# Other slot counts for the experts of a mixture-of-experts layer: 28 units of 128 slots in place of 32, in another order

## The chip, the cores and the metric

The program runs on one core of a Trainium2 chip. The metric is device time in microseconds (us) of one execution; smaller is better. Three runs of the kernel before took 2062.28, 2062.32 and 2063.19 us, so the median is 2062.32 us.

## The reference

Two transformer blocks on 256 tokens of 1024 features, in float32. The change concerns only the last part, the mixture of experts: each token goes to 8 of 64 experts, and each expert is a small gated network.

```python
def _moe(h, w_router_l, bias_l, w_gate_l, w_up_l, w_down_l, w_sh_gate_l, w_sh_up_l, w_sh_down_l):
    xt = h.reshape(t, d)                                     # 256 tokens x 1024
    scores = jax.nn.sigmoid(xt @ w_router_l)                 # 64 experts, in 8 groups
    biased = scores + bias_l
    # the best 4 groups, in them the best TOP_K = 8 experts: sel; weights from scores, summing to 2.5
    ...
    def expert_block(args):
        xe, e = args
        return (jax.nn.silu(xe @ w_gate_l[e]) * (xe @ w_up_l[e])) @ w_down_l[e]   # 1024 -> 256 -> 1024
    yb = lax.map(expert_block, (xb, block_e))
    routed = jax.ops.segment_sum(yb * slot_w, slot_tok)      # weighted sum per token
    shared = (jax.nn.silu(xt @ w_sh_gate_l) * (xt @ w_sh_up_l)) @ w_sh_down_l
    return routed + shared
```

An expert has 3 MB of weights (1024x256 gate, 1024x256 up, 256x1024 down), so the 64 experts bring 201 MB from HBM, whatever the routing.

## The kernel before

`route` scores the experts and sorts them by their load, which is the number of tokens that chose them. "Place" j is the j-th in that order; the first PRE = 2 places are always the experts 0 and 1, so that their weights can be loaded before the router is done. The later places' expert numbers are read into registers of the SyncE queue (L1772) and used as addresses of the loads.

The number of slots (tokens that an expert can take) is fixed when the program is built, by the place. TIERS says from which place on how many: 128 slots from place 0, 64 from place 12, 32 from place 40. If an expert had more tokens than its slots, `overflow` would send every token through every expert in a loop; a count on the chip decides that.

Slots are handled in **groups** of 256 and **units** of 128. A group is 2 experts of 128 slots, 4 of 64 or 8 of 32; each group is two units. For a group, `gather` copies the tokens of the 256 slots into columns with one-hot products on TensorE (tiles `oh`, `tok` to `xg`: 32 products of 128x256). For a unit, `experts` multiplies the gathered columns with the gate and up weights, 8 k-tiles for each expert, 512 columns each, into one PSUM tile (`pd<-ring,xg`). An expert of 64 or 32 slots uses 64 or 32 columns of TensorE's array and its own part of the output's partitions. `tail` makes the unit's scatter matrix and slot weights (`slT`, `w`), the activation (`tg`, then `h`), two transposes (`cst,h`, L1858), and the down products with 4 times 512 columns for each expert (`pm<-ring,hT`). `scatter` adds a group's two units to the output with 16 products (`pm<-y,PT`).

So a unit costs 12 float32 products of 512 columns for each of its 1, 2 or 4 experts. In the profile a float32 product of these shapes is two instructions (two passes), and is counted twice; gather and scatter products are one.

All expert weights come through one ring of NRING = 25 tiles of 128x1024 (512 KB), loaded by SyncE in the order of use (`ring`, L1576). An expert is 6 tiles: 4 of gate and up (`in_w_gu`), 2 of down (`in_w_ed`). Load k waits until the tile of load k - 25 has been used.

ORDER lists the tiers of the groups in the order in which they are taken. While a group's gate and up products run, `pump` puts in steps of the tail and scatter of the unit before and of the gather of the next group. A scheduler then fixes the order of instructions on each engine when the program is built, by its own estimate of when data arrive; the engine runs them in that order.

```python
TIERS = ((0, 128), (12, 64), (40, 32))
ORDER = (0, 2, 0, 0, 1, 1, 0, 1, 1, 0, 1, 2, 0, 1, 1, 2)
```

```python
m = P // nu                                   # columns of one expert in a unit of nu experts
for kk in range(2):
    k = 2 * c + kk
    for i, w in enumerate(ws):
        s0 = U["s0"] + i * m
        self.mm(U["ps"][i * m:(i + 1) * m], st["x"][:, k, s0:s0 + m], w[:, kk * 512:(kk + 1) * 512], k == 0, k == KD - 1)
```

Of the kernel before, what the change touches and what calls it, by code (L numbers as in the profile page):

```python
# [28 lines left out]
# ----------------------------------------------------------------- constants (of the shapes alone)  # L29
# [13 lines left out]
# places in the order by load: the first PRE are the experts 0.., then from each place on so many slots for each expert  # L43
PRE = 2
# lengths of streams, for the proportion in which they are merged
NCTX, PAD = 64, 4
NLAT, NWIN, NCONV = 70, 45, 120
# tiles of gates, of weights ahead; k-tiles that the vector engine takes; the group beside the shared expert's last product
# [4 lines left out]
TIERS = ((0, 128), (12, 64), (40, 32))  # L53
# the tiers of the groups of 256 slots, in the order in which they are taken
ORDER = (0, 2, 0, 0, 1, 1, 0, 1, 1, 0, 1, 2, 0, 1, 1, 2)
# [5 lines left out]
def _consts():  # L61
# [3 lines left out]
    # additive masks, queries on partitions  # L65
# [4 lines left out]
    # [partition t, free i]  # L70
# [4 lines left out]
    # within 32 rows and columns, lower and upper: the second block of a pair of s rows, the first of s columns  # L75
# [30 lines left out]
    # rope rows: 0..31 cos, 32..63 sin (with the sign), twice  # L106
# [23 lines left out]
# ----------------------------------------------------------------- layout of the inputs  # L130


def _pack(w, ncol):
    """(K, C) -> (C/ncol, 128, K/128 * ncol)"""
    k, c = w.shape
    return np.ascontiguousarray(w.reshape(k // P, P, c // ncol, ncol).transpose(2, 1, 0, 3)).reshape(c // ncol, P, -1)


def _cols(v):
    """(n*128,) -> (128, n)"""  # L140
    return v.reshape(-1, P).T
# [5 lines left out]
def _layout(inp):  # L147
# [50 lines left out]
    # second block  # L198
# [34 lines left out]
# ----------------------------------------------------------------- kernel  # L233


class Kern:
# [12 lines left out]
    # -------- streams of instructions: generators that yield where another stream may come in  # L249
# [20 lines left out]
    @staticmethod  # L270
    def merge(*streams):
        """streams: (generator, its number of steps); all advance in proportion"""
        live = [[g, 0, n] for g, n in streams]
        while live:
            e = min(live, key=lambda e: e[1] / e[2])
            e[1] += 1
            if next(e[0], StopIteration) is StopIteration:
                live.remove(e)
            yield

    # -------- small helpers
# [3 lines left out]
    def mm3(self, out, L, R, n, start=True, stop=True):  # L285
        """out = sum over n k-tiles of L[k]^T R[k]; L, R: (hi, lo) callables of k"""
# [19 lines left out]
    def split(self, hi, lo, src, lo_eng=None):  # L306
        """hi + lo = src exactly, each with at most 12 significant bits"""
        self.act(hi, src, AF.Copy)
        self.tt(lo, src, hi.bitcast(F32), ALU.subtract, lo_eng)

    def wraw(self, src, n):
        """src [128, n] in DRAM, loaded"""
# [6 lines left out]
    def wload(self, src, n, pre=True):  # L319
        """src [128, n] in DRAM -> hi, lo [128, n]"""  # L320
# [25 lines left out]
    # -------- setup  # L346
# [67 lines left out]
    def t5_bias(self, tp):  # L414
        """bias tiles [128 q, 8 heads, keys] with the masks added"""
# [5 lines left out]
        # differences of neighbouring buckets; bucket 0 keeps its value  # L421
# [4 lines left out]
        # three exact bf16 parts, block-diagonal over the key groups  # L426
# [12 lines left out]
        for b in range(2):  # L439
            nk = 32 if b == 0 else 64  # L440
            ng = 4 * nk
            for h0 in range(0, nk, 16):
# [10 lines left out]
                # ps columns (k, g, h) -> bias[q, h, g * nk + h0 + k]  # L453
# [6 lines left out]
    # -------- 1/sqrt(src * scale + eps), [128, n] for small n  # L460
# [13 lines left out]
    def rows(self, cols, dst):  # L474
        """dst [128, 256] = cols [128, 2] (tokens on partitions) as a row on every partition"""
# [6 lines left out]
    def rstd(self, sqs, n, name, dst=None):  # L482
        """1/sqrt(mean + eps) over the partitions of the [128, 256] tiles sqs: (columns [128, 2], rows [128, 256])"""
# [7 lines left out]
    def rstd_rows(self, sqs, n, tmp):  # L491
        """rows of 1/sqrt(mean + eps) over the partitions, worked out on every partition; tmp [128, 4, 256]"""
# [5 lines left out]
    def add_sq(self, acc, k, x, eng=None, **kw):  # L498
        """acc (+)= x^2, the first k writing it"""
# [10 lines left out]
    # -------- dense products; activations (hi, lo) [128, KT, 256]; calls cb(f, psum [128, n * 256], n)  # L510
# [3 lines left out]
    def dense_g(self, src, kt, nt, X, cb, m=P, kparts=1, per=1, pair=2):  # L514
        """out^T, features on partitions: nt tiles of m features. src(i): chunk i in DRAM [128, kt * per * m];
        kparts chunks of kt k-tiles each add up to one output, or one chunk holds per outputs.
        X: hi, lo, or one tile in float32"""
# [28 lines left out]
    # -------- softmax attention over up to 256 keys; score(b, h, ps) emits the products  # L546
    def attention(self, mp, *a):
        """stream: vtok [128, 2, w] tokens on partitions; head h's values at columns vcol(h); Y hi, lo [128, 4, 256]"""
# [47 lines left out]
    # -------- one layer of the first block  # L596
    def mix(self, l, XG, r):
        """x += mixer(x); hi, lo of x^T * g_mlp and the row of r^2 of its norm"""
        tp = lambda n: self.tc.tile_pool(name=f"{n}{l}", bufs=1, reuse_waits="tile")
        with tp("q") as qp:  # L600
# [7 lines left out]
            # output projection (the gates' halves come in here), residual  # L608
# [13 lines left out]
    def ff(self, l, XM, r, fp, res):  # L622
        """x += mlp(x), in two halves of the hidden features; res: the next XG and sums of squares"""
# [31 lines left out]
    def queries(self, l, XG, r, qp):  # L655
        """projections of the sliding-window attention"""
# [22 lines left out]
    def mixer(self, l, XG, Q, mp):  # L679
# [4 lines left out]
        # convolution branch: GLU, then the taps  # L684
# [20 lines left out]
        # sliding-window attention  # L705
# [9 lines left out]
        # latent attention: projections and norms of the latents  # L715
# [25 lines left out]
        # gates (tanh: 2 * sigmoid - 1) and the gated sum of the branches, which takes the first gate's place  # L741
# [15 lines left out]
        def branch(n, Y, f, gate):  # L757
            """outputs f, f + 1 of branch n"""
# [11 lines left out]
        # latent attention  # L770
# [50 lines left out]
        # layer norm over channels, swish  # L821
# [32 lines left out]
    def residual(self, k, X, g, acc, eng=None):  # L854
        """after x^T tile k is final: hi, lo of x*g and its part of the sum of squares"""
# [6 lines left out]
    # ---------------------------------------------------------------- second block  # L862
# [11 lines left out]
    def modulation(self, js, mp):  # L874
        """stream: parts js of the modulation, as columns [128, 8] each; 0, 1 for the context too (columns 48..63)"""
# [39 lines left out]
    def modulated(self, x, r, a, b, X, pool):  # L915
        """hi, lo of x * r * a + b; r rows, a and b columns per k-tile"""
# [6 lines left out]
    def decays(self, pool):  # L923
        """powers of the retention's decays: columns"""
# [8 lines left out]
    def decay_tables(self, pool):  # L933
        """DT [128 j, 4, 128 i], both directions; rows of powers"""
# [14 lines left out]
    def tr4(self, dst, srcs, scale=None):  # L949
        """dst [128, 4, 128] = transposes of four [128, 128] tiles, times scale(i) [128, 1]"""  # L950
# [11 lines left out]
    def rope2(self, dst, ps, f, scale, pool):  # L962
        """dst [128, 2, 256] = rotated ps (two heads), times scale"""
# [8 lines left out]
    def short_conv(self, z, ps, tile0, pool):  # L972
        """z [128, 2, 256] = 2 * silu(conv(ps)) of two channel tiles"""
# [12 lines left out]
    def l2(self, zs, pool, kt, ktok, mul):  # L986
        """z = 2 * silu; kt [128, 4, 256] (channels on partitions) and ktok [128, 2, 4, 128] of the normalised heads, times mul"""
# [12 lines left out]
    def state_features(self, X, base, pool, rope, F):  # L1000
        """stream: the features that feed the states, into the dict F"""
# [27 lines left out]
        # the decay gates first  # L1029
# [14 lines left out]
    def gdn_gates(self, p3, la, be, pool):  # L1044
        """la = -exp(a_log) * softplus(p + dt_bias), be = sigmoid(p)"""
# [6 lines left out]
        # softplus(x) = max(x, 0) + log1p(exp(-|x|)); log1p(e) = 2 atanh(e / (2 + e))  # L1052
# [16 lines left out]
    def b4(self, x):  # L1069
        """[128, 4] -> [128, 4, 128]"""  # L1070
        return x[:, :, None].to_broadcast([P, 4, P])
# [4 lines left out]
    def retention_kv(self, F, d, n, pool, kv):  # L1076
        """kv [PSUM 128 d, (4, 128 e)] of chunk n, direction d"""
# [12 lines left out]
    def gdn_prep(self, F, d, n, pool, kk, qk, G):  # L1090
        """stream: for chunk n in direction d the decays and the inverse of I + A, transposed, into the dict G;
        kk (and qk): the keys' products where A (the output's weights) may differ from 0"""
# [20 lines left out]
        # A, queries on partitions  # L1113
# [12 lines left out]
        # X, the inverse of I + A^T, and Y = X^T: blocks of 2 up to 32 in 32 columns, by X <- X - X B X  # L1126
# [28 lines left out]
        # the larger blocks: a, b the first and the second of a pair  # L1155
# [36 lines left out]
    def gdn_step(self, F, G, n, s_old, s_new, pool, o):  # L1192
        """stream: one chunk: s_new (None: not wanted) from s_old (None: zero); o: (output tile, whether to write or add)"""
# [42 lines left out]
    def context(self, c2):  # L1236
        """stream: states after the context: retention and delta rule, both directions"""
# [37 lines left out]
    def gdn_preps(self, F, pool, out, G):  # L1275
        """stream: gdn_prep for both directions of both chunks"""
# [24 lines left out]
    def head_norm(self, o, mean, pool):  # L1301
        """in place over the last axis of o [128, 2, 4, 128]: (o - mean) / sqrt(var + eps) or o / rms"""
# [14 lines left out]
    def final_norm(self, accs):  # L1317
        """rows of 1/rms of the first block's end, and of it times the next norm's, from sum((x g_final)^2)"""
# [24 lines left out]
    def mixer2(self, r1, r12, rffn):  # L1343
        nc, A, two, x = self.nc, self.A, self.two, self.xT
        tp = lambda n: self.tc.tile_pool(name=n, bufs=1, reuse_waits="tile")
        with tp("mb") as base:
# [7 lines left out]
            with tp("m1") as pool:  # L1354
# [19 lines left out]
                # retention: states, then the chunks  # L1374
# [29 lines left out]
            # delta rule  # L1404
            with tp("m2") as pool:
# [9 lines left out]
                # gates of the heads and of the merge beside it  # L1415
# [17 lines left out]
    def logits_x(self):  # L1433
        """the router's logits are r2 (x + r1 og) f_a W + f_b W: the parts of x and of f_b, and f_a W"""
# [16 lines left out]
    def mix_out(self, X, ro, go, rg, gz, gates, pool, rffn, wr, lx):  # L1451
        nc, A, two, x = self.nc, self.A, self.two, self.xT
        gates.append(pool.tile([P, 8, S], F32, name="gates1"))
        # norms over the heads, gates, transposed
# [14 lines left out]
        # merge; the factors 1/2 of silu and of the gates make 1/4  # L1469
# [13 lines left out]
        # og: the output o times its norm's gain; sums over the features of o^2, og^2 and og x  # L1483
# [41 lines left out]
        with self.tc.high_priority():  # L1525
            # sum((x + r1 og)^2) = sum(x^2) + r1 (2 sum(og x) + r1 sum(og^2))
# [540 lines left out]
```

## Time and profile before

| | us |
|---|---|
| median of three runs | 2062.32 |
| span of the profiled execution | 2062.9 |
| experts' stage, from the first product on an expert's weights to the last scatter | 1458.2 to 2050.3 |
| after it, last norm and store | 2050.3 to 2062.9 |

The profile gives no other time of the profiled execution than its span, which is 0.6 us above the median. Times in the rows are counted from the span's start. A TensorE instruction's end is modelled and overlaps the next, so what an instruction costs is read from the start of one row to the start of the next.

### The profile page before, as it was taken

The page shows a single profiled execution, that of the slowest core. Times are in us where ns is not written, and L with a number is a line of the kernel's source. Part 1 is how long each engine was busy: PE and PEld are TensorE (multiplying, and loading weights), DVE is VectorE, ACT ScalarE, POOL GpSimd, SP SyncE. Part 2 cuts the span into 40 slices and gives each one's busy share as a digit, 9 for nine tenths or more (in the row PEclk, how much of TensorE's full clock was granted, in tenths as well). Part 3 has the DMA queues.
Part 4 walks back from the last instruction along what each step waited for, and adds up shares of the span by engine and source line. Part 5 has one row for each costly group of instructions (what it writes and reads, how often), then busy time and mean ns, then how long its engine had stood idle before and what let it go on. Part 6 is the DMA issues. An engine that isn't in the chain of part 4 may idle for free. (4 is left out here: it accounts for less than half of the span.)

```text
span 2062.9 us, 38136 instructions
## 1 busy us (share of the span) xinstructions
PE 1900.5 (92%) x15189; PEld 1512.5 (73%) x15189; DVE 1272.2 (62%) x2464; ACT 786.7 (38%) x1397; POOL 292.4 (14%) x216
## 2 busy tenths in 40 slices
PE   5888999999888999998988998996999999999996
PEld 5787999999787999998987988895645443433432
DVE  7999787887986688578657864487222222222223
ACT  3246555344257555444444433352212121121111
POOL 3433210001334220011131121103000000000000
PEclk9989999999989999999989997896999999999998
DMA  4423556776423567655523522154798988889994
GB/s 160 124 82 113 171 177 201 244 245 200 134 76 106 176 202 228 210 172 172 156 91 96 161 91 65 33 180 186 264 409 305 353 276 304 283 287 409 348 349 197
DMA packets 122149, 414.49 MB, mean 201 GB/s; under 512 B 13936, under 2 KB 14832, under 8 KB 121968
## 3 DMA queue, kind: packets, MB, share of 16 engines
q1 hardware_dynamic: 120528, 409.92, 58.7%
q8 instruction: 120, 1.97, 0.4%
q10 hardware_dynamic: 1440, 2.11, 0.3%
q14 instruction: 61, 0.50, 0.1%
HBM read 410.92 MB, written 1.05 MB: 200 GB/s over the span
## 5 line engine op out<-in xcount | busy, mean ns | idle before, releaser
L283 PE MATMUL pd<-X,whi 128*128 128x256 f32 (+2 forms) x3280 | 639.3, 294 | 19.6 <-DVE X L304 9.8
L283 PEld LDWEIGHTS pd<-X,whi 128*128 128x128 f32 (+2 forms) x3280 | 534.0, 198 | 25.9 <-DVE X L304 11.7
L292 ACT ACTIVATE whi<-raw 128x1024 fp32r<-128x1024 f32 x340 | 356.4, 1051 | 458.7 <-PE pd L283 341.2
L283 PE MATMUL pd<-X,wlo 128*128 128x256 f32 (+2 forms) x1640 | 480.0, 293 | 8.2 <-POOL wlo L295 4.6
L295 DVE TENSOR_TENSOR wlo<-raw,whi 128x1024 fp32r<-128x1024 f32 x286 | 357.5, 1253 | 130.7 <-ACT whi L292 125.7
L283 PEld LDWEIGHTS pd<-X,wlo 128*128 128x128 f32 (+2 forms) x1640 | 324.7, 198 | 12.2 <-POOL wlo L295 6.1
L283 PE MATMUL pd<-ring,xg 128*64 128x512 f32 (+2 forms) x1024 | 284.3, 602 | 0.0
L283 PE MATMUL pd<-H,whi 128*128 128x256 f32 x1024 | 188.4, 286 | 0.3 <-ACT H L292 0.3
L295 DVE TENSOR_TENSOR y<-pm,y 128x512 fp32r<-128x512 f32 x64 | 44.2, 691 | 209.6 <-ACT y L292 209.5
L283 PEld LDWEIGHTS pd<-ring,xg 128*64 128x64 f32 (+2 forms) x1024 | 78.3, 136 | 113.4 <-issue 105.3
L295 POOL TENSOR_TENSOR wlo<-raw,whi 128x1024 fp32r<-128x1024 f32 (+1 forms) x54 | 132.6, 2470 | 197.6 <-ACT whi L292 197.2
L283 PEld LDWEIGHTS pd<-H,whi 128*128 128x128 f32 x1024 | 159.4, 192 | 1.1 <-ACT H L292 0.5
L283 PE MATMUL pm<-ring,hT 128*64 128x512 f32 (+2 forms) x512 | 153.7, 601 | 1.6 <-ACT hT L292 1.6
L304 DVE SCALAR_TENSOR_TENSOR cv<-up,vec,cv 128x256 f32<-128x256 f32 x240 | 148.1, 656 | 0.2
L283 PE MATMUL pd<-H,wlo 128*128 128x256 f32 x512 | 145.2, 284 | 0.4 <-DVE wlo L295 0.4
L304 DVE SCALAR_TENSOR_TENSOR acc<-rawm,sl,acc 128x512 f32<-128x512 f32 x112 | 94.1, 855 | 22.6 <-DMA rawm<-in_w_mod 22.2
L292 ACT ACTIVATE y<-pm 128x512 fp32r<-128x512 f32 (+1 forms) x66 | 39.4, 597 | 171.4 <-PE pm L283 171.4
L283 PEld LDWEIGHTS pd<-H,wlo 128*128 128x128 f32 x512 | 98.1, 192 | 0.8 <-DVE wlo L295 0.8
L283 PEld LDWEIGHTS pm<-ring,hT 128*64 128x64 f32 (+2 forms) x512 | 42.1, 136 | 75.1 <-issue 66.8
L283 PEld LDWEIGHTS pm<-oh,tok 128*128 128x128 f32 x512 | 67.2, 189 | 35.0 <-issue 29.3
L295 POOL TENSOR_TENSOR sqacc<-sqacc,sq 128x256 f32<-128x256 f32 x42 | 37.7, 905 | 366.0 <-ACT sq L292 364.9
L283 PE MATMUL pm<-oh,tok 128*128 128x256 f32 x512 | 87.3, 306 | 1.8 <-DVE oh L295 1.8
(515 smaller groups left out, 2721.6 us busy)
## 6 DMA issues: line engine op xcount, KB each, us to landing
ring<-in_w_gu SPq DMA_DIRECT2D x256, 512.0 KB, 6.8
ring<-in_w_ed SPq DMA_DIRECT2D x128, 512.0 KB, 8.5
raw<-in_w_up SPq DMA_DIRECT2D x64, 512.0 KB, 4.3
raw<-in_w_dn SPq DMA_DIRECT2D x64, 512.0 KB, 4.3
raw<-in_w_g SPq DMA_DIRECT2D x48, 512.0 KB, 3.6
rawm<-in_w_mod SPq DMA_DIRECT2D x96, 256.0 KB, 3.5
raw<-in_w_s SPq DMA_DIRECT2D x32, 512.0 KB, 3.7
raw<-in_w_x SPq DMA_DIRECT2D x32, 512.0 KB, 3.5
```

Source lines behind the costliest of these rows:

```text
L283: return self.nc.tensor.matmul(out, l, r, start=start, stop=stop)
L292: self.nc.scalar.activation(out, in_, f, **kw)
L295: (eng or self.nc.vector).tensor_tensor(out, a, b, op)
L304: self.nc.vector.scalar_tensor_tensor(out, a, s, b, op0, op1)
```

## The change

Two tables of constants. (The change also removes comments and docstrings, which leave blank lines behind, so that all line numbers stay.)

```diff
-TIERS = ((0, 128), (12, 64), (40, 32))
-# the tiers of the groups of 256 slots, in the order in which they are taken
-ORDER = (0, 2, 0, 0, 1, 1, 0, 1, 1, 0, 1, 2, 0, 1, 1, 2)
+TIERS = ((0, 128), (8, 64), (32, 32))
+
+ORDER = (0, 2, 0, 1, 1, 2, 0, 1, 1, 2, 0, 1, 1, 2)
```

| | experts before | units before | experts after | units after |
|---|---|---|---|---|
| 128 slots | 12 | 12 | 8 | 8 |
| 64 slots | 28 | 14 | 24 | 12 |
| 32 slots | 24 | 6 | 32 | 8 |
| all | 64 | 32 (16 groups) | 64 | 28 (14 groups) |

TensorE's order is the same up to the start of the fourth group, which is now one of 64 slots; the rows below are the first that differ (names: `pd` sums of gate and up, `ring` weights, `xg` gathered tokens, `hT` transposed activation, `oh`,`tok` gather).

```order
 L283 MATMUL pd<-ring,xg 128x512 x2
 L1858 MATMUL pm<-cst,h 128x128 x2
-L283 MATMUL pd<-ring,xg 128x512
+L283 MATMUL pd<-ring,xg 64x512
 L283 MATMUL pm<-ring,hT 128x512 x4
-L283 MATMUL pd<-ring,xg 128x512
-L283 LDWEIGHTS idb
-L283 MATMUL pm<-slT,idb 128x256
-L283 MATMUL pm<-oh,tok 128x256 x8
```

What moved: where a product of the next 128-slot expert stood, one of a 64-slot expert stands.

TensorE before, in the first unit of the second 32-slot group (the 12th group): a part of its gate and up products.

```order
L283 MATMUL pd<-ring,xg 32x512
L1858 MATMUL pm<-cst,h 128x128 x2
L283 MATMUL pm<-oh,tok 128x256 x8
L283 MATMUL pd<-ring,xg 32x512 x13
L283 MATMUL pm<-ring,hT 64x512
L283 MATMUL pm<-oh,tok 128x256 x7
L283 MATMUL pm<-ring,hT 64x512 x3
L283 MATMUL pm<-oh,tok 128x256
L283 MATMUL pd<-ring,xg 32x512 x8
L283 MATMUL pm<-ring,hT 64x512
```

TensorE now, in the second 32-slot group (now the 6th group): the second half of the first unit's gate and up products, and the first two of the second unit.

```order
L283 MATMUL pd<-ring,xg 32x512 x2
L1858 MATMUL pm<-cst,h 128x128 x2
L283 MATMUL pd<-ring,xg 32x512 x14
L283 MATMUL pm<-ring,hT 64x512 x5
L283 MATMUL pm<-y,PT 128x512 x4
L283 MATMUL pm<-ring,hT 64x512 x3
L283 MATMUL pm<-y,PT 128x512 x5
L283 MATMUL pd<-ring,xg 32x512
L283 MATMUL pm<-y,PT 128x512 x5
L283 MATMUL pd<-ring,xg 32x512
```

What moved: the 32-wide products still stand in stretches of several, broken by gather, scatter and down products, and some stand alone, but the stretches are cut in other places.

## Rows read from the trace of the kernel before

**Rows 1.** The page's first line.

```profile
span 2062.9 us, 38136 instructions
```

**Rows 2.** Stretches: us, then busy us (x instructions) per engine, granted clock, DMA share, GB/s.

```profile
1458.20:1516.80 58.60, 58.07 (x339) 27.03 (x337) 13.32 (x35) 14.80 (x27) 0.00 (x0) 1.00 0.85 307
1516.80:1555.10 38.30, 38.30 (x132) 17.03 (x132) 10.50 (x20) 4.65 (x10) 0.00 (x0) 1.00 1.03 409
...
1618.00:1652.50 34.50, 34.50 (x160) 14.30 (x156) 8.33 (x17) 7.22 (x14) 0.00 (x0) 1.00 1.01 378
...
1827.50:1884.60 57.10, 54.20 (x304) 19.80 (x303) 15.55 (x39) 9.80 (x19) 0.00 (x0) 1.00 0.88 337
1884.60:1918.20 33.60, 33.60 (x114) 14.00 (x113) 8.56 (x16) 4.95 (x9) 0.00 (x0) 1.00 1.03 409
1918.20:1950.10 31.90, 31.90 (x142) 13.72 (x141) 7.96 (x17) 5.67 (x11) 0.00 (x0) 1.00 0.91 338
1950.10:1988.80 38.70, 38.70 (x165) 15.07 (x164) 9.37 (x20) 6.64 (x14) 0.00 (x0) 1.00 0.91 326
1988.80:2050.30 61.50, 56.52 (x322) 20.20 (x322) 17.25 (x38) 11.22 (x23) 0.00 (x0) 1.00 0.74 286
2050.30:2062.90 12.60, 0.43 (x2) 0.00 (x0) 7.71 (x34) 1.95 (x6) 0.00 (x0) 0.55 0.23 86
```

**Rows 3.** Who TensorE, its weight loads and SyncE's queue waited for, 1458 to 2050.

```profile
PE pm L1858 <- DVE h L295: 6.1, 6, 1.7
...
PEld pd L283 <- DMA ring<-in_w_gu: 1.1, 2, 0.8
...
SPq L1576 <- PE pd L283: 173.9, 102, 9.2
SPq L1576 <- PE pm L283: 95.9, 90, 3.4
SPq L1576 <- DMA ring<-in_w_gu: 53.4, 75, 2.0
```

**Rows 4.** DMA in the same stretch.

```profile
DMA packets 52022, 189.77 MB, mean 321 GB/s; under 512 B 5776, under 2 KB 5776, under 8 KB 51984
```

**Rows 5.** TensorE in order of time, 128 slots: start, us, operation, passes.

```profile
1560.56 1.20 PE L283 MATMUL pm<-oh,tok 128*128 128x256 f32 x8
1561.61 0.30 PE L283 MATMUL pm<-w,ohb 128*128 128x1 bf16 x6
...
1571.79 1.10 PE L283 MATMUL pm<-y,PT 128*128 128x512 f32 x4
1572.73 1.88 PE L283 MATMUL pd<-ring,xg 128*128 128x512 f32 x4
...
1584.13 3.60 PE L283 MATMUL pm<-ring,hT 128*128 128x512 f32 x8
1587.56 2.89 PE L283 MATMUL pd<-ring,xg 128*128 128x512 f32 x10
```

**Rows 6.** The same, 64 slots.

```profile
1615.43 1.07 PE L283 MATMUL pd<-ring,xg 128*64 128x512 f32 x2
1616.43 0.30 PE L283 MATMUL pm<-w,ohb 128*128 128x2 bf16 x6
1616.66 1.94 PE L283 MATMUL pd<-ring,xg 128*64 128x512 f32 x8
1618.53 0.44 PE L1858 MATMUL pm<-cst,h 128*128 128x128 f32 x2
```

**Rows 7.** The same, 32 slots.

```profile
1870.05 3.64 PE L283 MATMUL pd<-ring,xg 128*32 128x512 f32 x32
1873.50 2.74 PE L283 MATMUL pm<-ring,hT 128*32 128x512 f32 x18
...
1877.17 1.04 PE L283 MATMUL pm<-ring,hT 128*32 128x512 f32 x2
1878.15 0.39 PE L283 MATMUL pm<-oh,tok 128*128 128x256 f32 x1
```

## The prediction

> **What bounds the kernel now.** The page's span is 2062.9 us [rows 1]; the change touches the experts' stage alone, so the next view is the sum by stretches, cut at the starts of groups [rows 2]. It shows TensorE busy in practically all of each stretch, at a granted clock of 1.00 (the upper of its two levels, 2.4 GHz), VectorE and ScalarE below half. DMA is busy too, 0.74 to 1.03. Which of the two sets the time is told by the waits [rows 3]: TensorE's weight loads waited 1.1 us for gate and up tiles; SyncE's queue waited 270 us for TensorE to free ring tiles (two rows), and in 75 places, 53 us, for an earlier load. So the loads wait for TensorE, hardly ever the reverse. TensorE works in a fixed order, so the stage, 2050.3 - 1458.2 = 592.1 us, is what that order costs.
>
> **What an instruction costs**, from one row's start to the next. A float32 product of 512 columns on the whole array: (1587.56 - 1584.13) / 4 = 0.86 us (8 passes are 4 products) [rows 5]. Experts of 64 slots: 8 passes, 4 products, take 1.87 us, so two run beside each other [rows 6]. Experts of 32 slots: 32 passes, 16 products, take 3.45 us, so four run beside each other [rows 7]. I call 0.86 us a *turn*: one product of 128 slots, up to two of 64, up to four of 32. A product that stands alone takes a whole turn: 1.00 us for 64 [rows 6], 0.98 for 32 [rows 7], 0.12 of it for the change of column width, or 0.11 a change with what the next instruction loses. A gather product takes 1.05 / 8 = 0.13, a scatter product 0.94 / 4 = 0.235 [rows 5].
>
> **The change, part by part.** Products by kind: 12 a unit and expert gave 144, 336 and 288 (128, 64, 32 slots), now 96, 288 and 384; the shared expert's 8 stay. If all ran in full turns, that would be 152 + 168 + 72 = 392 turns before and 104 + 144 + 96 = 344 after. But the order breaks the stretches. Counting in the order of both built programs (neighbours that write different partitions share a turn) gives 152 + 199 + 105 = 456 before and 104 + 178 + 136 = 418 now.
>
> - Turns: 38 fewer by 0.86 = -32.7 us.
> - Gather, two groups of 32 products: 64 by 0.13 = -8.3.
> - Scatter, two groups of 16: 32 by 0.235 = -7.5.
> - One-hot rows, slot weights and transposes of four units, at some 0.6 a unit by the short rows [rows 5, 6]: -2.5.
> - Changes of column width: 337 to 331, by 0.11: -0.7.
> - Waits for the activation `h` before the transposes, 6.1 us in 6 places now [rows 3]. They come where little stands between the slot weights (`w`) and the transposes, as in 32-slot units. Such places number five before and nine after in the order; two of the new ones have more cover than the old. At some 0.7 each: +2.8.
>
> Sum: -48.9 us. As a test, the same list prices the whole old order: 456 turns 392, gather 480 by 0.13 = 62, scatter 256 by 0.235 = 60, small ones 22, changes 37, together 574 of the 592.1 traced. The 18 left are waits, mostly in the last group, which is alike in both.
>
> ScalarE and VectorE lose two groups' evacuations; they are off the path, so that is worth nothing. The number of bytes is the same, and so are SyncE's loads of registers, one for each expert past the second. The last norm, 12.6 us, and all before the stage keep their order.
>
> Bounds. From above: piece the new sequence together from old stretches with the same neighbours [rows 2]. It is 0, 2 (58.6), 0 (38.3), then twice 1, 1, 2, 0 (31.9 + 38.7 + 57.1 + 33.6 = 161.3), then 1, 1, 2 (31.9 + 38.7 + 61.5 = 132.1): 551.6 us, or -40.5. The old 57.1 holds a worse-broken order than the new one, so I take the sum, and keep 2022 as the upper end of this case. From below: if the 18 us of waits shrink with the units, 28/32, and no `h` wait is added, -54; the span would be 2009.
>
> **Are the loads still covered?** An expert tile is 0.524 MB; at 409 GB/s, the rate of two whole stretches [rows 2], it takes 1.28 us. A repeating block of the new order (0, 1, 1, 2) holds 108 tiles, 138.5 us of DMA. TensorE's time without the first three groups, which stay (58.6 + 38.3), is about (592.1 - 48.9 - 96.9) / 3 = 149 us a block. So the loads fit, with 10 us to spare a block. Within the 32-slot group alone they don't: 48 tiles are 61.6 us, TensorE needs some 47. There the ring has to cover the difference of 15 us: 25 tiles are 32 us ahead, and the two 64-slot groups before refill it. The old 12th group did just this in 57.1 us with DMA at 0.88 and no wait for it. I count no stall.
>
> The Trainium skill (DMA: Bandwidth & Descriptors, the section on where 436 GB/s comes from) says that loads from HBM are bound by HBM's share of some 358 GB/s for a core, not by the fabric's 435. By that rule a block would be 56.6 MB / 358 = 158 us, 9 over TensorE's, three times: an estimate of 2041 us. The trace doesn't agree: two stretches ran at 409 GB/s.
>
> The Trainium skill (TensorEngine Tiling (Array Packing), Theoretical Speedup) gives up to 2x for 64 columns and up to 4x for 32. Full turns would save 392 - 344 = 48 instead of 38, 8.6 us more. Rows 7 show four beside each other, but only where the order leaves them adjacent.
>
> **The rivals.**
>
> 1. *Fully packed turns.* The stage gains 48 turns: 2013.4 - 8.6 = 2005 us. For it: the stretch of 32 passes [rows 7]. Against: the lone products, which the new order has as well. Chance 0.04.
> 2. *Loads bind, mildly.* DMA holds less than 409 GB/s over a whole block and TensorE waits at the end of each 32-slot group. At a rate between two rows of 64-slot groups, (378 + 338) / 2 = 358 GB/s [rows 2], a block takes 158 us, and each of three is 9 us longer: 2041. (The Trainium skill's HBM share, above, comes out at the same.) For it: a mean of 190 MB / 543 us = 350 GB/s is now asked for, 321 before [rows 4]. Against: 409 in two stretches. Chance 0.05.
> 3. *Loads bind, hard: slower.* The 326 to 338 GB/s of the 64-slot stretches, with DMA engines 0.91 busy [rows 2], would be all that such loads can do. A block is then 56.6 MB / 332 = 170 us, 21 more than TensorE's, three times 21 = 63: 2076 us. It decides below 56.6 / 165 us = 343 GB/s. For it: the busy share near 1. Against: in those stretches SyncE was waiting for TensorE, and 378 GB/s stands in another 64-slot stretch. Chance 0.02.
> 4. *Gain eaten by waits.* Every 64- and 32-slot unit, 20 of them, would have to wait 2.4 us more for `h`, against 1.7 for the longest now [rows 3]: 2062, no change. Chance 0.02.
> 5. *The change doesn't do what it says:* an expert overflows. The ninth place must not exceed 64 tokens, nor the 33rd place 32. The reference's router on its inputs gives 55 and 27. Otherwise all experts run again, at least 384 loads by 1.28 = 492 us: about 2500. Chance 0.01.
>
> **How the numbers follow.** The forecast, TensorE's order without new stalls, has 0.86: span 2062.9 - 48.9 = 2014.0, and as the median of runs lies 0.6 below the span, 2013.4; I say 2013. Its own range is 2007 to 2022. The range given, 2004 to 2024, takes in fully packed turns below, and above a little of the mild DMA case. A change of 0.2% is 4 us, about what a measurement of this kernel can tell from none. Faster: 0.86 + 0.04 + 0.05 = 0.95. Within: 0.02 (the fourth rival). Slower: 0.02 + 0.01 = 0.03.
>
> **What would show it.** Right: the stage starts at 1458 as before and lasts some 543 us; the passes of 128*128 products fall by 96, those of 128*64 by 96, those of 128*32 rise by 192; TensorE busy in every stretch at clock 1.00; DMA mean near 350 GB/s; the wait for `h` at 8 to 10 us; SyncE still waiting for TensorE, though less. Wrong: rows "PE or PEld <- DMA ring" of more than a few us, placed in or after the 32-slot groups, with DMA at full share (the loads bind); 32-slot stretches far above 47 us; or instructions of the overflow loop (L1924 on).

## The result

The changed kernel takes 2016.22 us (median of 4 runs, 2008.36 to 2023.35) against 2062.3; the ratio is 0.9767, 95% interval 0.9736 to 0.9798. Forecast were 2013 us and a range of 2004 to 2024.

The profiled execution has a span of 2017.8 us, 45.1 less than before [rows 1]. Its stretches, cut at starts of groups as in [rows 2] (us, then busy us (x instructions) of TensorE, its weight loads, VectorE, ScalarE, GpSimd; granted clock, DMA share, GB/s):

```profile
span 2017.8 us, 37799 instructions
```

```profile
1459.00:1517.50 58.50, 57.97 (x338) 26.99 (x336) 13.33 (x35) 14.81 (x27) 0.00 (x0) 1.00 0.85 309
1517.50:1556.00 38.50, 38.50 (x133) 17.02 (x132) 10.51 (x20) 4.79 (x10) 0.00 (x0) 1.00 1.03 409
1556.00:1590.10 34.10, 34.10 (x148) 14.87 (x147) 9.93 (x21) 6.58 (x13) 0.00 (x0) 1.00 0.95 348
1590.10:1629.80 39.70, 39.70 (x176) 16.11 (x172) 10.55 (x23) 7.50 (x15) 0.00 (x0) 1.00 0.92 340
1629.80:1680.50 50.70, 47.38 (x284) 17.66 (x283) 12.68 (x32) 9.32 (x18) 0.00 (x0) 1.00 0.97 363
1680.50:1714.10 33.60, 33.60 (x115) 13.97 (x115) 8.56 (x16) 4.95 (x9) 0.00 (x0) 1.00 1.03 410
...
1785.60:1838.00 52.40, 49.08 (x284) 18.01 (x283) 12.69 (x32) 9.31 (x18) 0.00 (x0) 0.97 0.98 370
...
1942.20:2005.30 63.10, 58.11 (x323) 20.38 (x322) 17.27 (x38) 11.18 (x23) 0.00 (x0) 0.97 0.72 278
2005.30:2017.80 12.50, 0.38 (x2) 0.00 (x0) 7.72 (x34) 1.95 (x6) 0.00 (x0) 0.57 0.23 87
```

The first three groups and the last norm are as they were; the stage is 2005.3 - 1459.0 = 546.3 us instead of 592.1. So 45.8 us went from the stage, and 0.8 came back before it, where the code is the same. A 32-slot group between others took 57.1 us before and takes 50.7 and 52.4. DMA is now at 0.92 to 1.03 from the third group to the last but one, and at 0.72 in the last. The waits in the stage, against [rows 3]:

```profile
PE pm L1858 <- DVE h L295: 8.1, 9, 1.7
...
PEld pd L283 <- DMA ring<-in_w_gu: 3.5, 8, 0.8
PEld pd L283 <- DMA ring<-in_w_ed: 2.9, 7, 0.8
...
SPq L1576 <- PE pd L283: 153.6, 91, 7.0
SPq L1576 <- DMA ring<-in_w_gu: 65.0, 97, 2.3
SPq L1576 <- PE pm L283: 58.9, 77, 3.4
```

SyncE's queue still waits mostly for TensorE to free tiles, 212.5 us (two rows) instead of 270; the loads waited for each other a little more often. TensorE's products were idle for 12.1 us of the stage in all, and none of these waits ended with a tile. Its weight loads have 6.8 us put down to tiles (the two rows shown and one of 0.4). These are not waits for the loads: counting the landed tiles and the products off in order, every tile of the stage had landed some 5 us or more before its product. So TensorE's order is still the bound. DMA's mean rose from 321 [rows 4] to 344 GB/s (347 in the stage alone; the window here ends 5 us after it):

```profile
DMA packets 52067, 189.90 MB, mean 344 GB/s; under 512 B 5790, under 2 KB 5790, under 8 KB 52029
```

### The profile page after: what moved, and what is told of

Its sections match the earlier page's. It is cut to its first block, busy times and chain, and to the rows that moved or that the text cites. A ratio compares the mean times of both kernels' runs of the same rounds, so it can differ in the third digit from the quotient of the medians.

```text
span 2017.8 us, 37799 instructions
## 1 busy us (share of the span) xinstructions
PE 1851.2 (92%) x15061; PEld 1482.0 (73%) x15061; DVE 1253.8 (62%) x2428; ACT 773.1 (38%) x1371; POOL 293.1 (15%) x216
## 5 line engine op out<-in xcount | busy, mean ns | idle before, releaser
L283 PE MATMUL pd<-ring,xg 128*32 128x512 f32 (+2 forms) x1024 | 255.3, 608 | 0.0
L283 PEld LDWEIGHTS pd<-H,whi 128*128 128x128 f32 x1024 | 161.5, 194 | 1.8 <-ACT H L292 1.1
L283 PE MATMUL pm<-ring,hT 128*32 128x512 f32 (+2 forms) x512 | 153.3, 613 | 0.5 <-ACT hT L292 0.5
L295 DVE TENSOR_TENSOR y<-pm,y 128x512 fp32r<-128x512 f32 x56 | 38.7, 691 | 183.1 <-ACT y L292 183.1
L283 PEld LDWEIGHTS pd<-ring,xg 128*32 128x32 f32 (+2 forms) x1024 | 68.2, 130 | 107.3 <-issue 95.4
L292 ACT ACTIVATE y<-pm 128x512 fp32r<-128x512 f32 (+1 forms) x58 | 34.6, 597 | 171.7 <-PE pm L283 171.7
L283 PEld LDWEIGHTS pm<-ring,hT 128*32 128x32 f32 (+2 forms) x512 | 38.4, 131 | 70.4 <-issue 63.6
L283 PEld LDWEIGHTS pm<-oh,tok 128*128 128x128 f32 x448 | 59.2, 189 | 38.4 <-issue 28.9
L295 DVE TENSOR_TENSOR macc<-macc,pm 128x512 f32<-128x512 f32 x56 | 38.1, 687 | 66.9 <-PE pm L283 66.9
```

The source lines that it names most:

```text
L283: return self.nc.tensor.matmul(out, l, r, start=start, stop=stop)
L292: self.nc.scalar.activation(out, in_, f, **kw)
L295: (eng or self.nc.vector).tensor_tensor(out, a, b, op)
```

## The experiments

Two theories were to be told apart. *Order*: the stage costs what TensorE's built order costs, by turns, gathers, scatters and changes of column width. *Loads*: the stage is limited by what DMA brings, so that the change works only as far as DMA has room. In what follows "priced" means this list of prices applied to an order (with 0.118 us for a gather product, 0.11 for a change of width and some 0.5 for the short rows of a unit): 563 us for the kernel before, 513 for the changed one. That is 29 and 33 us less than the two stages took, so a difference of two prices is what can be compared. The turns that the list counts in the built orders are in the traces too: passes that start together give 456 and 418.

**The changed kernel again**, six more runs.

> The changed kernel once more, unaltered. The one profile of it shows 45.7 us less in the experts' stage, 3.2 us less of a gain than the 48.9 forecast, and two windows of 3.4 us at half clock inside the stage, at 1819 and 1990, where the kernel before has none. Clock theory: such windows explain the miss and the wide spread of the runs (2008 to 2023); a new profile shows them in other numbers, each costing about 1.7 us, and the time goes with the mean granted clock, 0.945 for the slowest and 0.956 for the fastest run. Rival (loads bind now and then): the clock is the same and TensorE's waits for ring tiles grow from the 7 us of the first profile to 15 or more in a slow run.

Measured: 2012.48 us (2005.91 to 2019.92), ratio 0.9776 (0.9752 to 0.98). All before the stage, the stage, and the third of its four 32-slot groups:

```profile
0.00:1452.00 1452.00, 1311.17 (x12548) 1258.88 (x12549) 1107.23 (x2082) 672.20 (x1176) 292.68 (x216) 0.94 0.49 154
1452.00:1998.20 546.20, 534.05 (x2515) 217.49 (x2513) 140.42 (x312) 98.63 (x189) 0.00 (x0) 0.99 0.92 347
1778.20:1828.80 50.60, 47.28 (x287) 18.11 (x287) 12.92 (x33) 9.53 (x19) 0.00 (x0) 1.00 0.98 371
```

The stage took 546.2 us again, while what lies before it took 1452.0 instead of 1459.0. The 7.2 us between the two profiled executions (2012.47 and 2019.69) are thus not the stage's. Before the stage the clock records of the traces have TensorE at the lower level for 177 us here and for 191 in the first profile; half of the difference is 6.8 us. So the clock theory was right that the clock makes this difference, but wrong on where. It was right on the lower clock inside the stage: that 32-slot group took 50.6 us at a clock of 1.00 and 52.4 at 0.97 in the first profile, with the same instructions. Here the fall stands in the last group, 6.8 us in all as in the first profile, so the stage comes out the same. Loads that bind now and then show in neither profile; the slowest run (2023.35) was not profiled.

**One half alone: 128 slots for 8 places, 32 slots from place 40 as before** (30 units).

```diff
-TIERS = ((0, 128), (8, 64), (32, 32))
-ORDER = (0, 2, 0, 1, 1, 2, 0, 1, 1, 2, 0, 1, 1, 2)
+TIERS = ((0, 128), (8, 64), (40, 32))
+ORDER = (0, 2, 0, 1, 1, 1, 0, 1, 1, 2, 0, 1, 1, 1, 2)
```

> One half of the change alone: 128 slots only for the first 8 places as now, but 32 slots only from place 40 as before; 30 units. Order theory (a turn 0.86 us, counted in the built order): 443 turns against 418 now and 456 before, one gather and one scatter more than now; the whole order is priced 33 us over the changed kernel, 17 under the kernel before, so 2049. Rival (a unit costs the same whatever its slots, 46 us for 4 units): 23 us under before, 2039. Loads rival: fewer tiles are asked for per time, nothing to see.

Measured: 2046.41 us, ratio 0.9935 (0.9909 to 0.996). **The other half alone**: `TIERS = ((0, 128), (12, 64), (32, 32))`, `ORDER = (0, 2, 0, 0, 1, 2, 0, 1, 0, 1, 2, 0, 1, 1, 2)`, also 30 units.

> The other half alone: 128 slots for the first 12 places as before, 32 from place 32 on as now; 30 units. Order theory: 433 turns, priced 19 us over the changed kernel, so 2035, 27 under before. Rival (equal price for a unit): 2039. Rival (loads bind around the 32-slot groups): 2040 or more with TensorE waiting for ring tiles after each of the four.

Measured: 2030.41 us, ratio 0.9863 (0.9838 to 0.9888). The two stages, first kernel and second:

```profile
1453.20:2033.30 580.10, 568.88 (x2578) 231.79 (x2577) 149.93 (x330) 105.46 (x202) 0.00 (x0) 0.99 0.89 327
```

```profile
1448.60:2007.10 558.50, 548.30 (x2579) 234.13 (x2577) 150.21 (x330) 105.70 (x202) 0.00 (x0) 1.00 0.91 340
```

Both have 30 units and 15 groups, yet their stages differ by 21.6 us. An equal price for a unit is out; the turns and widths priced them 14.3 us apart in the same sense (443 against 433 turns, 361 changes against 308). The first half alone was priced 33 us over the changed kernel and was 33.8 over it (580.1 against 546.3); the second 19 over, and was 12.2. Of the 7 us that are missing there, 3.4 are the clock: it was at 1.00 throughout that stage, while the other two stages have 6.8 us at the lower level each. The rest, 3.4 us, is the list's, and nothing tried here says of which price.

**The experts of a unit kept adjacent** (the same edit at the down products, L1867).

```diff
-                        for i, w in enumerate(ws):
+                        for i, w in reversed(list(enumerate(ws))):
                             s0 = U["s0"] + i * m
-                            self.mm(...)
+                            q = self.mm(...)
+                            if i < nu - 1:
+                                self.tc.keep_in_program_order(q)
```

> The changed kernel with the experts of a unit kept adjacent: for each k-tile the product on the tile that lands last comes first and the others are pinned behind it. The order now has all turns full: 344 against 418, 205 changes of column width against 331. Order theory without a limit from the loads: 77 us less, 1939. With the loads at 409 GB/s as the limit: a block (0, 1, 1, 2) has 123 us of TensorE and 138.5 of loads, so the stage cannot be much under 474 us and, with the start that TensorE sets, some 488: 1960, with TensorE waiting for ring tiles for tens of us. Rival (loads hold 358 GB/s): the stage is 554 us, 2025, slower than the changed kernel. Rival (turns don't matter, a unit's price does): 2016, no change.

Measured: 1959.52 us (1956.06 to 1964.78), ratio 0.9517 (0.9496 to 0.9537), the fastest of all with the whole computation. TensorE in order of time (start, us, operation, passes, what ended an idle time), and four of the stage's stretches:

```profile
1639.65 1.90 PE L283 MATMUL pd<-ring,xg 128*32 128x512 f32 x16
1641.37 1.90 PE L283 MATMUL pm<-ring,hT 128*32 128x512 f32 x16
...
1655.96 1.88 PE L283 MATMUL pd<-ring,xg 128*128 128x512 f32 x4
1658.56 1.92 PE L283 MATMUL pm<-ring,hT 128*32 128x512 f32 x16 [0.71 <-DMA ring<-in_w_ed]
```

```profile
1450.00:1500.00 50.00, 48.77 (x279) 24.58 (x281) 10.93 (x28) 13.59 (x25) 0.00 (x0) 1.00 0.80 283
1500.00:1550.00 50.00, 50.00 (x253) 23.50 (x246) 16.00 (x34) 9.68 (x19) 0.00 (x0) 1.00 1.03 409
...
1750.00:1800.00 50.00, 40.25 (x268) 17.06 (x270) 13.55 (x33) 9.54 (x18) 0.00 (x0) 0.93 1.03 408
...
1850.00:1900.00 50.00, 46.31 (x267) 18.67 (x264) 13.16 (x30) 10.00 (x19) 0.00 (x0) 1.00 1.02 407
```

```profile
PE pm L1860 <- DVE h L295: 16.5, 13, 1.8
...
PE pm L283 <- DMA ring<-in_w_ed: 9.6, 6, 3.4
PEld pd L283 <- DMA ring<-in_w_gu: 6.5, 10, 4.0
PEld pm L283 <- DMA ring<-in_w_ed: 4.7, 3, 4.1
...
PE pd L283 <- DMA ring<-in_w_gu: 3.1, 1, 3.1
```

```profile
SPq L1576 <- DMA ring<-in_w_gu: 147.7, 213, 1.5
SPq L1576 <- DMA ring<-in_w_ed: 71.7, 105, 1.4
SPq L1576 <- PE pd L283: 35.7, 37, 7.0
SPq L1576 <- PE pm L283: 26.1, 69, 1.5
```

The 32-slot products now stand in stretches of 16 passes, 1.72 us for 8 products, and there are no lone ones. TensorE is idle a fifth of the stretch at 1750 (of the 9.8 us, 6.1 end with a tile's landing) while DMA runs at 407 to 409 GB/s from 1500 to 1900. SyncE's queue now waits 219 us behind earlier loads and 62 us for TensorE, the reverse of the changed kernel: here the loads bind, and they bind at 409. The stage is 491 us (priced 436 by the order), as forecast (488) for loads at that rate. At 358 GB/s its 189.8 MB alone would have taken 530.

**Packed, with half of the loads** (the packed kernel and this edit, the second line also at the down products).

```diff
-        return self.ring(self.A[name][e, :, c * WCH:(c + 1) * WCH]...)
+        return self.ring(self.A[name][e, :, c * WCH:c * WCH + 512]...)
-    ... w[:, kk * 512:(kk + 1) * 512] ...
+    ... w[:, 0:512] ...
```

> The packed kernel with half of each expert tile loaded and used for both k-tiles (half of the experts' weights is left out). Its order costs TensorE the same as the packed one (344 turns both; the list prices it 438 us against 435). If the loads bind the packed kernel, as its windows at 408 to 409 GB/s from 1500 to 1900 say, the stage falls from 491 us to the order's price and some 25 to 30 us of waits, 463 to 468, so 1932 to 1938. If the packed kernel is bound by its waits for h and by the lower clock instead, nothing changes: 1960.

Measured: 1924.84 us, ratio 0.9339 (0.9305 to 0.9373). Its stage, then the packed kernel's:

```profile
1449.90:1911.00 461.10, 455.32 (x2515) 203.95 (x2513) 140.27 (x312) 99.81 (x191) 0.00 (x0) 0.99 0.64 207
```

```profile
1450.70:1941.30 490.60, 456.72 (x2514) 206.50 (x2513) 139.52 (x312) 99.90 (x192) 0.00 (x0) 0.98 0.98 387
```

```profile
PE pm L1860 <- DVE h L295: 3.5, 2, 1.8
```

TensorE is busy for the same 455 to 457 us. With 207 instead of 387 GB/s moved, the stage is 29.5 us shorter, nearly all of it idle time of TensorE (33.9 us in the packed kernel, 5.8 here): 12.7 us of its products' waits for tiles are gone, and 13.0 us of their waits for `h` (last fence). So the packed kernel loses time to its loads, as its rates say. How much is theirs this run doesn't settle, because the scheduler made another order for the half-size loads (231 changes of width instead of 205): whether the waits for `h` went with the loads or with the order is not shown.

**The changed kernel with half of the loads** (the same edit without the packing).

> The changed kernel with half of each expert tile loaded (256 KB instead of 512) and used for both k-tiles, so the experts' weights are half left out. Same products. If the loads bound the changed kernel, its time falls by more than TensorE's order does. The scheduler makes another order from it, 357 turns against 418, priced 63 us less: order theory 1953, and no wait for ring tiles. Loads rival: below 1945.

Measured: 1942.28 us, ratio 0.9433 (0.9402 to 0.9463), stage 471.7 us. By the letter this speaks for the loads (below 1945). By its rows it doesn't: the scheduler, presumably because it takes half-size loads as landing sooner, made an order with 357 turns and 237 changes, priced 63 us less. Of the 12 us beyond that, 6.4 are idle time of TensorE that went (12.1 to 5.8 us), 4.6 of them waits for `h` (8.1 to 3.5). None of it was a wait for a tile in either kernel. The other 5 us were not tried further.

**The kernel before with its experts kept adjacent.**

> The kernel before with the experts of a unit kept adjacent, as in the packed run of the changed kernel. Order theory: 392 turns against 456, the whole order priced 67 us less, 1995, and the loads, 138 us a block of 149 us or more, still covered. Rival (turns don't matter): 2062.

Measured: 2011.75 us, ratio 0.976 (0.9732 to 0.9788); a gain as large as the change's own, but 17 us short of the forecast. Its stage, and a wait:

```profile
1461.70:2003.70 542.00, 522.08 (x2643) 239.84 (x2641) 157.74 (x348) 113.57 (x217) 0.00 (x0) 0.98 0.93 350
```

```profile
PE pm L1860 <- DVE h L295: 13.1, 11, 1.9
```

Three things the price list doesn't hold: the wait for `h` doubled (6.1 to 13.1 us; that denser products leave less to cover it is likely, but not tried), products waited 2.8 us for tiles, and the clock stood at 0.98 in the stage, at most 11 us of 542, where the kernel before had 1.00. Together they are 21 us at most, enough for the 17. On the packed order the change itself is worth 2011.75 - 1959.52 = 52 us.

**Groups sorted by tier**: `ORDER = (0, 0, 0, 0, 1, 1, 1, 1, 1, 1, 2, 2, 2, 2)`.

> The changed kernel's tiers with the groups sorted: four groups of 128 slots, six of 64, then the four of 32 slots in a row, so that 192 of the 384 expert tiles are needed in the last four groups. TensorE's order alone is priced 30 us under the changed kernel (392 turns): 1986. Loads at 409 GB/s: after the first ten groups, 300 us, some 171 tiles are still to land, 219 us, then 14 us of work: stage 533, 2006, with TensorE waiting for ring tiles for some 30 to 50 us in the last four groups. Loads at 358 GB/s: 250 us instead of 219, 2037.

Measured: 2028.71 us, ratio 0.9839 (0.9802 to 0.9876). The last four groups, a stretch within, and waits for tiles:

```profile
1770.80:2018.30 247.50, 226.31 (x1152) 73.39 (x1140) 53.00 (x122) 32.55 (x63) 0.00 (x0) 0.99 0.98 385
```

```profile
1900.00:1950.00 50.00, 43.07 (x200) 9.61 (x199) 8.47 (x22) 3.33 (x7) 0.00 (x0) 1.00 1.03 409
```

```profile
PEld pd L283 <- DMA ring<-in_w_gu: 30.3, 39, 1.4
...
PEld pm L283 <- DMA ring<-in_w_ed: 18.5, 20, 1.9
...
PE pd L283 <- DMA ring<-in_w_gu: 4.9, 20, 0.5
...
PE pm L283 <- DMA ring<-in_w_ed: 3.5, 11, 0.9
```

This is what a kernel bound by loads looks like: weight loads wait 49 us for tiles while DMA moves 405 to 409 GB/s (from 1800 to 2000). The products themselves waited only 8.4 us for tiles; in the trace, passes that start together give 426 turns, not the 392 of the built order, as if products that wait for their tiles one by one no longer ran beside each other. The order's price alone (1986) fails; the forecast with loads (2006) missed by 23: the first ten groups took 313.8 us, not 300, and the last four 247.5, not 233. So the interleaved ORDER is what keeps the changed kernel clear of this.

**A ring of 17 tiles**: `NRING = 17`.

> The changed kernel with 17 ring tiles instead of 25, so the loads run 10 us less ahead. In the profile of the changed kernel the tile that came closest was used 5 us after it had landed, in the groups of 32 slots 8 to 11 us. Order theory: 421 turns, priced 3 us more, 2019, plus the few us by which the closest tiles are late in the four 32-slot groups: 2019 to 2035. Loads rival (the ring barely covers): each block is 10 us longer, 2046 or more.

Measured: 2022.05 us, ratio 0.982 (0.9796 to 0.9845).

```profile
PEld pd L283 <- DMA ring<-in_w_gu: 12.8, 18, 1.3
PEld pm L283 <- DMA ring<-in_w_ed: 3.9, 4, 1.7
```

The stage is 554.8 us, 8.5 more than the changed kernel's; its order is priced 3 us more, and its clock was 1.00 throughout, worth 3.4 us. So late tiles cost some 9 us. Waits put down to tiles grew from 6.8 to some 18 us on the weight loads. Counted off in order as above, the last three 32-slot groups now have tiles that land just when their products start. A ring a third smaller costs little; 25 tiles cover the loads with something to spare.

## Why the prediction was right

- *What bounds it.* TensorE's order did, before and after: in neither stage did a product wait for a tile, and tiles of the changed kernel landed some 5 us or more ahead. SyncE's queue waited for TensorE 270 us before and 212.5 after, and 84 and 105 us behind earlier loads (gate and up, down, shared). In the packed kernel, which the loads bind, it is 62 against 220.
- *The terms.* Turns, gathers, scatters, short rows and widths were forecast at 51.7 us less. The two halves of the change, each with its own order, came out 34 and 12 us over the changed kernel where the list said 33 and 19: the first confirms the prices, the second is 7 us off, half of it by the clock. Counting the turns in the built order was the step that mattered: full turns would have been 392 and 344, and were 456 and 418; with 48 turns less instead of 38 the forecast would have been 8.6 us lower.
- *Waits for `h`.* Forecast +2.8 us, measured +2.0 (6.1 to 8.1) in 9 places instead of 6.
- *The miss.* The stage fell by 45.8 us, not 48.9. The term that was left out is the clock: in the changed kernel's 32-slot groups it fell in two places (0.97 in two stretches, 0.03 of 52.4 and of 63.1 us, together 3.5 us); the same group at 1.00 took 1.7 us less. In the kernel before no such fall stands between 1458 and 2050. The prediction took the clock of 1.00 as given, and named it as a sign of being right; that sign failed. That the time came within 4 us of 2013 is in part luck: single runs lie from 2006 to 2023 us, and the time before the stage alone differs by 13 us between profiles.
- *Loads still covered.* Right, and by more than was said. The two 32-slot groups between others took 50.7 and 52.4 us (forecast some 47) where their tiles need 61.6; the ring carried the difference. But the 149 us a block is wrong: it is the time of eleven groups over three, while three blocks (0, 1, 1, 2) are twelve, as the third group was taken off as well. With only the first stretch off it is (592.1 - 48.9 - 58.6) / 3 = 161.5, and measured were 163.0 and 157.5 for the first two. So 19 us or more a block were to spare, not 10. The 123 us a block that the packed run's expectation gives TensorE have the same slip: (546.3 - 77 - 58.5) / 3 are 137, only just under its loads (138.5).
- *The limit of 358 GB/s* (the Trainium skill, DMA: Bandwidth & Descriptors): here the page's sentence and the traces differ. The packed kernel held 407 to 409 GB/s for 400 us on one core, and its time is the one forecast for 409, not for 358. The page works its 358 out as half of an HBM stack's rate, for two cores; whether another core on the same memory would change the rate, no run here shows. The time of the changed kernel decided nothing on this: by the right length of a block, 158 us of loads at 358 GB/s would have fitted too, or nearly, so the 2041 of the second rival does not follow from its condition, and the 2076 of the third would be some 2040. The packed kernel is what tells them apart.
- *Fully packed turns* (the Trainium skill, TensorEngine Tiling (Array Packing), Theoretical Speedup): the factor of 4 holds in the packed trace, 1.72 us for 8 products of 32 slots, which is 0.215 a product against 0.86; the factor of 2 stands in [rows 6]. The prediction gave this rival 8.6 us because it compared savings; for the changed kernel itself 74 turns were still to be had, and with all turns full its stage lost 56 us more (546.3 to 490.6) before the loads bound it.
- *Overflow* did not occur: the loop's lines (L1924 to L1952) have no instructions in the trace.

## What to carry to other kernels

Where several narrow products share the array, count how many really stand side by side in the built order; a scheduler that places each by its own estimate of when data arrive can undo the sharing (418 turns here where 344 do), and putting the product on the last-landing tile first, with the others pinned behind it, restores it. Before taking work off one engine, work out what the next one (here DMA at 409 GB/s) needs for the same stretch: the change stayed clear of it by 19 us or more a block, the packed version ran into it. When blocks are priced, count that the time and the work belong to the same groups. A price list from one trace, applied to the new order's counts, gave the change of the stage to 3 us of 46.

## What the hardware showed unasked

The time before the experts' stage, the same instructions in all kernels, varied from profile to profile:

```profile
0.00:1448.60 1448.60, 1307.80 (x12548) 1255.53 (x12549) 1105.03 (x2082) 672.52 (x1176) 291.84 (x216) 0.94 0.49 154
```

```profile
0.00:1461.70 1461.70, 1319.03 (x12549) 1266.40 (x12550) 1105.31 (x2082) 672.64 (x1176) 292.82 (x216) 0.93 0.49 153
```

VectorE and ScalarE are busy for the same time in both; TensorE is busy 11 us longer in the second. The clock records have the lower level for 167 us in the first and 195 in the second, and half of the difference is 14 us. So the 13 us between these two executions go with how long the full clock was granted, and single times of this kernel tell less than its stage in a profile. Inside the stage the clock was 1.00 throughout in the kernel before. In other kernels it fell in places where TensorE had been idle in short pieces: in the packed kernel to 0.93 in the stretch at 1750, in which it was busy for 40.25 of 50 us. Such pieces did not always bring it down: the last group of the kernel before was busy for 56.52 of 61.5 us at 1.00 [rows 2].
